# Layer 0's opening in a two-layer encoder trunk: squares and their sums placed behind the last input chunk, two weight units split into idle tiles, and another bank for the fourth projection block

## The chip, the cores and the metric

The kernel runs on one core of one Trainium2 chip. The metric is the device time of one execution in microseconds (us). The core has five engines: TensorE (PE; its weight loads are shown as PEld), VectorE (DVE), ScalarE (ACT), GpSimd (POOL) and SyncE (SP), which here only issues DMAs. Each engine works its own list of instructions in order and waits on semaphores for the others.

## The reference

Input x is 512 x 1024 (float32), the depth is 2. Cut to what matters here:

```python
for l in range(DEPTH):
    h = rmsnorm(x, attn_norm[l])                    # x * rsqrt(mean(x*x) + EPS) * g
    proj = jnp.einsum('bsd,de->bse', h, w_in[l])    # 1024 -> 6 x 512
    sb_q, sb_k, sb_v, df_q, df_k, df_v = jnp.split(proj, splits, axis=-1)
    sb_out = stick_breaking_attention(sb_q, sb_k, sb_v)          # 8 heads of 64
    dq, dk = rope(df_q, pos), rope(df_k, pos)
    df_out = rmsnorm(differential_attention(dq, dk, df_v, lam), subln_norm[l]) * (1.0 - lambda_init)
    x = x + jnp.einsum('bse,ed->bsd', concat([sb_out, df_out]), w_o[l])
    h = rmsnorm(x, mlp_norm[l])
    u = jnp.square(jax.nn.relu(jnp.einsum('bsd,df->bsf', h, w_ff1[l])))   # 1024 -> 4096
    x = x + jnp.einsum('bsf,fd->bsd', u, w_ff2[l])
return rmsnorm(x, final_norm)
```

## The kernel before, in words

**Layout.** x is held transposed: eight chunks of 128 features (partitions) by 512 tokens. The gain g is applied to x before the projections, and the factor rsqrt(mean) of each token is applied to the products when they are evicted from PSUM. So the projections need only x and g; the row `rbc` (the factors, on all partitions) is needed at the first eviction.

**Three products for one.** Each float32 operand is split into a high part (a rounded copy, type fp32r) and a low part (operand minus high part). `three` (L255 to L260) issues three matmuls for one: high by high (L258), and the two mixed ones (L259, L260). For x this split is `make_h` (L208 to L212): ScalarE writes h_hi (L209), VectorE h_lo (L210). For weights it is `split_part` (L110 to L119): ScalarE writes whi (L118), VectorE wlo (L119).

**Weights.** They come from HBM in units of 128 x 1024 in a fixed order: three raw buffers (pool wraw), and two pairs of split tiles (whi, wlo; pool wspl). A unit's DMA can be issued once the split that read its raw buffer is done, and a unit can be split once the matmuls that used its split tile are done. `W.next` splits two units ahead in program order. The first units of layer 0 are 0 and 1 (block d0, its q and k halves), 2 (w0v), 3 and 4 (d1q, d1k), 5 (w1v), 6 and 7 (d2), 8 (w2v).

**The opening of layer 0.** The DMAs of x's eight chunks and of quarters of units 0 and 1 are issued in turn. For each chunk ScalarE and VectorE make h and, for every second chunk, a quarter of both units. TensorE takes d0's two products together, chunk by chunk (48 matmuls into two banks), then block by block w0v, d1q, d1k, w1v and on (24 matmuls each). The sum of squares `ssq` is made beside it by `add_sq` (L214 to L223): ScalarE squares chunk 0 into ssq (L216) and each other chunk into a tile sq (L222), GpSimd adds sq to ssq (L223).

**The norm.** `rms_a` (L225 to L246) transposes ssq on TensorE (rs_a), reduces on VectorE (L230, L231), takes the power -0.5 on GpSimd (L236), splits the factors (chi, clo) and spreads them on diagonals (dgha, dgla: L241, L243). `rms_b` (L248 to L253) multiplies these with ones on TensorE (rb_a) and ScalarE copies the result to rbc. `RA` and `RB` count chunks of projections (a step is one `three`): in layer 0 rms_a is issued at step 21, rms_b at step 26. Until then finished blocks are held in their PSUM banks; after it cos_t and sin_t are multiplied by rbc, and the held blocks are evicted: `evict_d` (u, v, rotated on GpSimd L459 and L460, split, moved by DMAs on SP's queue L425 and copied by ScalarE L446 into the stacks st and kl) and `evict_v` (tv, transposed on TensorE as vT).

**Banks.** Three PSUM banks have the tag mm, two s, two t, one o. d0 and w0v take the three mm banks; the block that starts at step 24 (d1q) takes an s bank, and d1k waits for the bank of d0's q. The s banks later hold the attention scores.

**Attention** of layer 0 runs between the projections, shared out by cost. The scores S0d (L487, L488) use the s banks, which are free again when ScalarE has read them in the exponentials p0d (L540). md_hi and md_lo, four slices of 512 columns each, receive the differential heads after their norm.

**Order.** The order of instructions on each engine is made by a scheduler when the kernel is built, from the program order, its own costs and the dependencies.

Of the kernel before, what the change touches and what calls it, by code (L numbers as in the profile page):

```python
# [9 lines left out]
F32 = mybir.dt.float32  # L10
F32R = mybir.dt.float32r
BF16 = mybir.dt.bfloat16
AF = mybir.ActivationFunctionType
ALU = mybir.AluOpType
# [8 lines left out]
KC = D // P  # L23
# [8 lines left out]
LAG2, LAG3, KSB = 2, 3, 7  # L32
MTB = 1
FB = 6
SQP = False
RST = 2
WARM = 10
RA, RB, DLY_V = (21, 8), (26, 16), 3.5
MAN = ()
_CTX = {}  # L40
KC_GAP = 0.9
# [45 lines left out]
class _Weights:  # L87
    def __init__(self, nc, dram, rawp, splp):
        self.nc, self.dram, self.rawp, self.splp = nc, dram, rawp, splp
        self.loaded = self.split = self.used = 0  # L90
        self.raw, self.tiles = {}, {}
        self.depth = 3

    def parts(self, i):
# [14 lines left out]

    def split_part(self, i, a, b):  # L110
        nc = self.nc
        if i not in self.tiles:
            hi = self.splp.tile([P, 1024], F32R, tag="whi", name=f"whi{i}")
            lo = self.splp.tile([P, 1024], F32R, tag="wlo", name=f"wlo{i}")
            self.tiles[i] = (hi, lo)
        hi, lo = self.tiles[i]
        raw = self.raw[i]
        nc.scalar.activation(hi[:, a:b], raw[:, a:b], AF.Copy)  # L118
        nc.vector.tensor_tensor(out=lo[:, a:b], in0=raw[:, a:b], in1=hi[:, a:b].bitcast(F32), op=ALU.subtract)  # L119

    def do_split(self, n):
        while self.split < min(n, len(_UNITS)):
# [7 lines left out]
    def next(self, kind):  # L130
        i = self.used
        assert _UNITS[i][0] in kind
        self.used += 1
        if i > 0:
            self.do_split(i + 2)
        return self.tiles.pop(i)
# [3 lines left out]
def trunk(ctx, tc, xT, w, gains, lamv, cos, sin, out):  # L140
    nc = tc.nc
# [5 lines left out]
    def bank(tag, name, bufs=2):  # L147
        return ps.tile([P, 512], F32, tag=tag, name=name, bufs=bufs)
# [3 lines left out]
    W = _Weights(nc, w, wraw, wspl)  # L152
    cp.tile([P, 96], F32, tag="lead", name="lead")
    x = cp.tile([P, KC, S], F32, tag="x", name="x")
    h_hi = cp.tile([P, KC, S], F32R, tag="h_hi", name="h_hi")
    h_lo = cp.tile([P, KC, S], F32R, tag="h_lo", name="h_lo")
    ssq = cp.tile([P, S], F32, tag="ssq", name="ssq")
# [32 lines left out]
    def gcol(which, l, c):  # L190
        i = {"attn": l * 8, "mlp": 16 + l * 8, "final": 32, "sub": 40 + l}[which] + c
        return g_all[:, i : i + 1]
# [13 lines left out]
        nc.vector.tensor_tensor(out=lo, in0=src, in1=hi.bitcast(F32), op=ALU.subtract)  # L206

    def make_h(c, g):  # L208
        nc.scalar.activation(h_hi[:, c, :], x[:, c, :], AF.Copy, scale=g)  # L209
        nc.vector.scalar_tensor_tensor(  # L210
            out=h_lo[:, c, :], in0=x[:, c, :], scalar=g, in1=h_hi[:, c, :].bitcast(F32),
            op0=ALU.mult, op1=ALU.subtract)  # L212

    def add_sq(c, first, sqt, eng=nc.gpsimd, sqe=None):  # L214
        if first:
            nc.scalar.activation(ssq, x[:, c, :], AF.Square)  # L216
            return
        sq = sqt("sq")
        if sqe is not None:
            sqe.tensor_mul(sq, x[:, c, :], x[:, c, :])  # L220
        else:
            nc.scalar.activation(sq, x[:, c, :], AF.Square)  # L222
        eng.tensor_tensor(out=ssq, in0=ssq, in1=sq, op=ALU.add)  # L223

    def rms_a(src, inv_n, col, name, eng, dgt):  # L225
        pt = bank("t", "rs_" + name)
# [21 lines left out]
    def rms_b(bc, name, dg):  # L248
        dg_hi, dg_lo = dg
        pb = bank("t", "rb_" + name)  # L250
        nc.tensor.matmul(pb, ones_r.to_broadcast([P, P]), dg_hi, start=True, stop=False)
        nc.tensor.matmul(pb, ones_r.to_broadcast([P, P]), dg_lo, start=False, stop=True)
        nc.scalar.copy(bc, pb)  # L253

    def three(pt, a, b, first, last):  # L255
        ah, al = a
        bh, bl = b
        nc.tensor.matmul(pt, ah, bh, start=first, stop=False)  # L258
        nc.tensor.matmul(pt, ah, bl, start=False, stop=False)  # L259
        nc.tensor.matmul(pt, al, bh, start=False, stop=last)  # L260

    def hpair(c):
        return h_hi[:, c, :], h_lo[:, c, :]

    def wpair(u, c, n=P):
        return u[0][:, c * n : (c + 1) * n], u[1][:, c * n : (c + 1) * n]

    def block(name, tag="mm"):
        pt = bank(tag, name, 3 if tag == "mm" else 2)
        u = W.next("px" if name[0] == "p" else "1")  # L270
        for c in range(KC):
            three(pt, wpair(u, c), hpair(c), c == 0, c == KC - 1)
            yield pt if c == KC - 1 else None

    def constants(a2):
        nc.sync.dma_start(cos_t, cos)
        nc.sync.dma_start(sin_t, sin)
        lam_in = a2.tile([P, L * 4 * 64], F32, tag="t", name="lam_in", bufs=4)
        nc.sync.dma_start(lam_in, lamv.partition_broadcast(P))
        lam4 = lam_in.rearrange("p (l j d) -> p l j d", l=L, j=4)  # L280
        lam_pr = a2.tile([P, L, 2, 128], F32, tag="t", name="lam_pr", bufs=4)[:, :, :, 0:64]
        for l in range(L):
            for m in range(2):
                nc.vector.tensor_mul(lam_pr[:, l, m, :], lam4[:, l, 2 * m, :], lam4[:, l, 2 * m + 1, :])
                nc.vector.tensor_reduce(out=lam_sm[:, l, m : m + 1], in_=lam_pr[:, l, m, :], axis=AX.X, op=ALU.add)
        nc.scalar.activation(lam_ex.rearrange("p l m -> p (l m)"), lam_sm.rearrange("p l m -> p (l m)"), AF.Exp)
        for l in range(L):
            li = 0.8 - 0.6 * math.exp(-0.3 * l)
            nc.vector.tensor_sub(nlam[:, l : l + 1], lam_ex[:, l, 1:2], lam_ex[:, l, 0:1])
            nc.vector.tensor_scalar_add(nlam[:, l : l + 1], nlam[:, l : l + 1], -li)  # L290
            nc.vector.tensor_scalar_mul(gsub[:, l : l + 1], gcol("sub", l, 0), 1.0 - li)
# [57 lines left out]
    for l in range(L):  # L349
        with ExitStack() as actx:  # L350
# [3 lines left out]
            md_hi = ap_.tile([P, 4, S], F32R, tag="mdh", name=f"mdh{l}")  # L354
            md_lo = ap_.tile([P, 4, S], F32R, tag="mdl", name=f"mdl{l}")
# [19 lines left out]
            if l == 0:  # L375
                for c in range(KC):
                    if c % 2 == 0:
                        for i in range(2):
                            W.split_part(i, c * P, (c + 2) * P)
                    make_h(c, gcol("attn", 0, c))  # L380
                W.split = 2
                for c in range(KC):
                    add_sq(c, c == 0, tt, nc.gpsimd, nc.gpsimd if c % 2 and SQP else None)
                constants(a2)

            def evict_v(pt, kind, b, which):
# [306 lines left out]
            def dense():  # L693
                step, held = 0, []
                if l == 0:
                    b = int(ORDER[0][1])
                    us = [W.next("x"), W.next("x")]
                    pts = [bank("mm", f"p0{i}", 3) for i in range(2)]
                    for c, i in [(c, i) for c in range(5) for i in range(2)] + [(c, i) for i in range(2) for c in (5, 6, 7)]:
                        three(pts[i], wpair(us[i], c), hpair(c), c == 0, c == KC - 1)  # L700
                        step += 1
                        yield 3 * 0.216
                    held = [(pts[0], "d", b, "q"), (pts[1], "d", b, "k")]
                for item in ORDER[1 if l == 0 else 0 :]:
                    kind, b = item[0], int(item[1])
                    for which in ("qk" if kind in "ds" else "v"):
                        name = f"p{l}{kind}{b}{which}"
                        for pt in block(name, "s" if step == 24 else "mm"):
                            step += 1
                            if step == RA[l]:  # L710
                                dgs["a"] = rms_a(ssq, 1.0 / D, rcol, f"a{l}", nc.vector, tr)
                            if step == RB[l]:
                                rms_b(rbc, f"a{l}", dgs["a"])
                                nc.vector.tensor_mul(cos_t, cos_t, rbc)
                                nc.vector.tensor_mul(sin_t, sin_t, rbc)
                            yield 3 * 0.216
                        held.append((pt, kind, b, which))
                        if step >= RB[l]:
                            for args in held:
                                {"w": evict_v, "u": evict_v, "s": evict_s, "d": evict_d}[args[1]](*args)  # L720
                            held = []
                yield from wo(1)
# [4 lines left out]
            for cost in dense():  # L727
# [5 lines left out]
                while live and credit > 0:  # L733
                    c = next(at, None)
# [15 lines left out]
        with ExitStack() as fctx:  # L750
# [25 lines left out]
            for half in range(2):  # L776
                us = []
                for f in range(HC):
                    step = 0
# [6 lines left out]
                    if half == 0 and f == 0:  # L786
                        first = pt
# [5 lines left out]
                for db in range(KC):  # L793
                    pt = bank("mm", f"f2_{l}{half}{db}", 3)
                    for s in range(2):
                        u = W.next("2")
                        for f in range(n // 2):
                            g = s * (n // 2) + f
# [70 lines left out]
```

## Time and profile before

| | |
|---|---|
| time, median of 3 runs (lowest, highest) | 1233.09 us (1231.47, 1233.61) |
| time of the profiled execution | 1232.63 us |
| its span | 1230.8 us |
| granted TensorE clock, mean | 0.993 |
| busy: TensorE, VectorE, ScalarE, GpSimd | 1196.4, 683.6, 550.6, 210.9 us |
| GpSimd's additions L223 of the opening (7), busy | 10.1 us |
| the opening's h_lo L210 (8), busy | 9.5 us |
| d0's last matmul starts | 24.12 us |
| w0v's and d1q's last matmuls start | 31.13, 37.06 us |
| first exponential p0d | 59.05 us |

Busy time is the time in which an engine carries out instructions, and for TensorE it contains matmuls that run into each other. A row in order of time gives start, duration, engine, line, operation, what it writes and reads, and in brackets how long the engine was idle before it and who ended that wait. The waits are given as: who waited, for whom, total us, number, longest. The windows give the busy time of each engine between two times.

### The profile page before, as it was taken

The numbers are of one execution on the slowest core, as the hardware profiler recorded it, in microseconds if no ns is written. First come the engines' busy times: TensorE is split into PE (matmuls) and PEld (weight loads), VectorE is DVE, ScalarE is ACT, GpSimd is POOL, SyncE is SP. The second block draws the span as 40 slices with busy tenths as digits, with TensorE's granted clock in tenths as the row PEclk, the third lists the DMA queues.
The fourth block names the chain that finished last, engine by engine and source line by source line (L and its number), as shares of the span: only waits on it lengthen the run. The fifth ranks groups of instructions, "written<-read, shape, count | busy, mean of one in ns | idle before, by whom it ended". The sixth has DMA issues, their size and how long they took to land.

```text
span 1230.8 us, 15320 instructions
## 1 busy us (share of the span) xinstructions
PE 1196.4 (97%) x5658; PEld 989.4 (80%) x5658; DVE 683.6 (56%) x1009; ACT 550.6 (45%) x932; POOL 210.9 (17%) x267
## 2 busy tenths in 40 slices
PE   8999999999999999999998999999999999999996
PEld 4777888888888888888887788788888888888886
DVE  6687878765442244443367787887644323444325
ACT  5666566544332134333246765665443221433214
POOL 4223453230000000001123244432200000000002
PEclk9999999999999999999999999999999999999998
DMA  6444444123322323323324343432232233233221
GB/s 198 114 142 121 115 134 122 59 86 103 103 88 101 103 88 101 103 87 102 103 84 141 105 134 107 129 92 84 86 103 99 90 103 95 93 103 91 90 94 69
DMA packets 46890, 128.16 MB, mean 104 GB/s; under 512 B 7264, under 2 KB 10336, under 8 KB 46816
## 3 DMA queue, kind: packets, MB, share of 16 engines
q1 hardware_dynamic: 46672, 127.17, 33.8%
q8 instruction: 45, 0.74, 0.2%
q14 instruction: 29, 0.24, 0.1%
q10 hardware_dynamic: 144, 0.02, 0.0%
HBM read 104.09 MB, written 2.10 MB: 86 GB/s over the span
## 4 chain that ended last, share of the span: by engine, by line
PE 87%; DVE 4%; ACT 3%; POOL 2%; issue 1%; DMA 1%; SPq 0%; DVEq 0%; POOLq 0%; ACTq 0%
PE f L258 19%; PE f L259 19%; PE f L260 19%; PE wo L259 2%; PE wo L258 2%; PE wo L260 2%; DVE wlo L119 1%; PE T1s L568 1%; PE T0s L568 1%; ACT p0d L540 1%; PE O1s L597 0%; PE O0s L597 0%; PE O0s L596 0%; PE O1s L596 0%; PE S1d L487 0%
## 5 line engine op out<-in xcount | busy, mean ns | idle before, releaser
L118 ACT ACTIVATE whi<-raw 128x1024 fp32r<-128x1024 f32 (+2 forms) x200 | 205.1, 1027 | 493.3 <-PE f L259 427.6
L119 DVE TENSOR_TENSOR wlo<-raw,whi 128x1024 fp32r<-128x1024 f32 (+2 forms) x200 | 247.7, 1239 | 151.6 <-ACT whi L118 150.5
L258 PE MATMUL f<-h_hi,whi 128*128 128x512 f32 x512 | 199.4, 389 | 0.0
L260 PE MATMUL f<-h_hi,wlo 128*128 128x512 f32 x512 | 199.2, 389 | 0.0
L259 PE MATMUL f<-h_lo,whi 128*128 128x512 f32 x512 | 199.2, 389 | 0.0
L258 PE MATMUL f<-uh,whi 128*128 128x512 f32 x496 | 192.9, 389 | 0.0
L259 PE MATMUL f<-ul,whi 128*128 128x512 f32 x496 | 192.9, 389 | 0.0
L260 PE MATMUL f<-uh,wlo 128*128 128x512 f32 x496 | 192.9, 389 | 0.0
L771 DVE SCALAR_TENSOR_TENSOR ft<-f,rbc 128x512 f32<-128x512 f32 x64 | 44.3, 692 | 163.9 <-PE f L260 163.0
L258 PEld LDWEIGHTS f<-h_hi,whi 128*128 128x128 f32 x512 | 96.1, 188 | 20.0
L260 PEld LDWEIGHTS f<-h_hi,wlo 128*128 128x128 f32 x512 | 96.1, 188 | 20.0
L259 PEld LDWEIGHTS f<-h_lo,whi 128*128 128x128 f32 x512 | 96.1, 188 | 19.8
L223 POOL TENSOR_TENSOR ssq<-ssq,sq 128x512 f32<-128x512 f32 x28 | 44.5, 1591 | 382.1 <-ACT sq L222 372.7
L260 PEld LDWEIGHTS f<-uh,wlo 128*128 128x128 f32 x496 | 93.1, 188 | 19.5
L258 PEld LDWEIGHTS f<-uh,whi 128*128 128x128 f32 x496 | 93.1, 188 | 19.3
L259 PEld LDWEIGHTS f<-ul,whi 128*128 128x128 f32 x496 | 93.1, 188 | 19.2
L800 DVE TENSOR_TENSOR x<-x,f 128x512 f32<-128x512 f32 x32 | 22.0, 688 | 103.0 <-PE f L260 103.0
L340 POOL TENSOR_TENSOR ssq<-ssq,sqf 128x256 f32<-128x256 f32 x6 | 4.4, 738 | 338.4 <-ACT sqf L338 335.0
L206 DVE TENSOR_TENSOR ul<-fu,uh 128x512 fp32r<-128x512 f32 x64 | 44.1, 692 | 0.4 <-ACT uh L205 0.4
L205 ACT ACTIVATE uh<-fu 128x512 fp32r<-128x512 f32 x64 | 40.6, 634 | 2.0
L772 ACT ACTIVATE fu<-ft 128x512 f32<-128x512 f32 x64 | 39.6, 618 | 1.6 <-DVE ft L771 1.6
L508 POOL TENSOR_TENSOR sig0s<-sig0s,C0s 128x128 f32<-128x128 f32 (+3 forms) x32 | 30.1, 939 | 55.0 <-DVE C0s L505 39.0
(722 smaller groups left out, 2164.9 us busy)
## 6 DMA issues: line engine op xcount, KB each, us to landing
raw<-in_w SPq DMA_DIRECT2D x176, 512.0 KB, 3.4
raw<-in_w SPq DMA_DIRECT2D x16, 448.0 KB, 3.2
x<-in_xT SPq DMA_DIRECT2D x8, 256.0 KB, 4.5
out_xT<-y SPq DMA_DIRECT2D x8, 256.0 KB, 2.4
raw<-in_w SPq DMA_DIRECT2D x8, 128.0 KB, 4.5
cos_t<-in_cos SPq DMA_DIRECT2D x2, 256.0 KB, 4.2
sin_t<-in_sin SPq DMA_DIRECT2D x2, 256.0 KB, 4.3
kl0d0k<-l0d0k SPq DMA_DIRECT2D x8, 64.0 KB, 2.2
```

What stands on the lines that cost most here:

```text
L118: nc.scalar.activation(hi[:, a:b], raw[:, a:b], AF.Copy)
L119: nc.vector.tensor_tensor(out=lo[:, a:b], in0=raw[:, a:b], in1=hi[:, a:b].bitcast(F32), op=ALU.subtract)
L205: nc.scalar.activation(hi, src, AF.Copy)
L206: nc.vector.tensor_tensor(out=lo, in0=src, in1=hi.bitcast(F32), op=ALU.subtract)
L223: eng.tensor_tensor(out=ssq, in0=ssq, in1=sq, op=ALU.add)
L258: nc.tensor.matmul(pt, ah, bh, start=first, stop=False)
L259: nc.tensor.matmul(pt, ah, bl, start=False, stop=False)
L260: nc.tensor.matmul(pt, al, bh, start=False, stop=last)
L508: nc.gpsimd.tensor_mul(sig[:, 0:wd], sig[:, 0:wd], C[:, 1 : wd + 1])
L568: nc.tensor.transpose(pt[:, off : off + P], u["w"][qi][:, kb * P : (kb + 1) * P], ident)
L771: nc.vector.scalar_tensor_tensor(out=t, in0=pt, scalar=0.0, in1=rbc, op0=ALU.max, op1=ALU.mult)
L772: nc.scalar.activation(uu, t, AF.Square)
```

## The change

The seven additions of squares in layer 0's opening go from GpSimd to VectorE. `behind` writes order dependencies without a semaphore: the first square stands behind the last h_hi on ScalarE, the first addition behind the last h_lo on VectorE, the squares are kept in their order, and the third square and second addition stand behind the split of unit 2. Units 2 and 3 are split within the opening, and their split tiles are the two halves of md_hi and md_lo of layer 0 (`home`) instead of whi and wlo. rms_b of layer 0 is issued at step 30 instead of 26. The block that starts at step 32 (d1k) takes an s bank too. The switch SQP, which was off, is removed. Layer 1 and the other uses of `add_sq` keep GpSimd.

```diff
-SQP = False
-RA, RB, DLY_V = (21, 8), (26, 16), 3.5
+RA, RB, DLY_V = (21, 8), (30, 16), 3.5
...
-        self.raw, self.tiles = {}, {}
+        self.raw, self.tiles, self.home = {}, {}, {}
...
     def split_part(self, i, a, b):
         nc = self.nc
+        if i not in self.tiles and i in self.home:
+            self.tiles[i] = self.home[i]
         if i not in self.tiles:
...
-        nc.scalar.activation(hi[:, a:b], raw[:, a:b], AF.Copy)
-        nc.vector.tensor_tensor(out=lo[:, a:b], in0=raw[:, a:b], in1=hi[:, a:b].bitcast(F32), op=ALU.subtract)
+        h = nc.scalar.activation(hi[:, a:b], raw[:, a:b], AF.Copy)
+        self.last = h, nc.vector.tensor_tensor(
+            out=lo[:, a:b], in0=raw[:, a:b], in1=hi[:, a:b].bitcast(F32), op=ALU.subtract)
...
+    def behind(a, b):
+        tc.add_manual_dep(a.ins, b.ins.name, mybir.DependencyInfo(
+            mybir.DependencyClass.NoSync, mybir.DependencyReason.DATA), reason="order")
...
-                    make_h(c, gcol("attn", 0, c))
+                    ends = make_h(c, gcol("attn", 0, c))
                 W.split = 2
-                for c in range(KC):
-                    add_sq(c, c == 0, tt, nc.gpsimd, nc.gpsimd if c % 2 and SQP else None)
+                for i in range(2):
+                    W.home[2 + i] = tuple(
+                        m[:, 2 * i : 2 * i + 2, :].rearrange("p e t -> p (e t)") for m in (md_hi, md_lo))
+                squares = [add_sq(c, c == 0, tt, nc.vector) for c in range(KC)]
+                behind(squares[0][0], ends[0])
+                behind(squares[1][1], ends[1])
+                for a, b in zip(squares[1:], squares):
+                    behind(a[0], b[0])
+                W.do_split(3)
+                behind(squares[2][0], W.last[0])
+                behind(squares[2][1], W.last[1])
+                W.do_split(4)
                 constants(a2)
...
-                        for pt in block(name, "s" if step == 24 else "mm"):
+                        for pt in block(name, "s" if step in (24, 32) else "mm"):
```

`add_sq` and `make_h` now return their two instructions, so that `behind` can name them.

More of the change, by code (lines that the diff above doesn't have):

```diff
@@ L208, in make_h, with add_sq @@
     def make_h(c, g):
-        nc.scalar.activation(h_hi[:, c, :], x[:, c, :], AF.Copy, scale=g)
-        nc.vector.scalar_tensor_tensor(
+        a = nc.scalar.activation(h_hi[:, c, :], x[:, c, :], AF.Copy, scale=g)
+        return a, nc.vector.scalar_tensor_tensor(
             out=h_lo[:, c, :], in0=x[:, c, :], scalar=g, in1=h_hi[:, c, :].bitcast(F32),
             op0=ALU.mult, op1=ALU.subtract)
-    def add_sq(c, first, sqt, eng=nc.gpsimd, sqe=None):
+    def add_sq(c, first, sqt, eng=nc.gpsimd):
         if first:
-            nc.scalar.activation(ssq, x[:, c, :], AF.Square)
-            return
+            return nc.scalar.activation(ssq, x[:, c, :], AF.Square), None
         sq = sqt("sq")
[L219 to L223, printed above, removed]
+        s = nc.scalar.activation(sq, x[:, c, :], AF.Square)
+        return s, eng.tensor_tensor(out=ssq, in0=ssq, in1=sq, op=ALU.add)
+    def behind(a, b):
+        tc.add_manual_dep(a.ins, b.ins.name, mybir.DependencyInfo(
+            mybir.DependencyClass.NoSync, mybir.DependencyReason.DATA), reason="order")
     def rms_a(src, inv_n, col, name, eng, dgt):
```

## The prediction

> **What bounds the kernel now.** I read the page first: TensorE is busy for 97% of the span, so an edit pays only where TensorE stands still or runs on late operands. The windows by stage come next, then the order in time of each engine from 0 to 65 us.
>
> ```profile
> PE 1196.4 (97%) x5658; PEld 989.4 (80%) x5658; DVE 683.6 (56%) x1009; ACT 550.6 (45%) x932; POOL 210.9 (17%) x267
> ```
> Windows of the opening (busy us of PE, PEld, DVE, ACT, POOL; granted clock; DMA share; GB/s):
> ```profile
> 5.00:10.00 5.00, 4.13 (x15) 2.21 (x13) 3.09 (x5) 3.86 (x9) 1.40 (x3) 1.00 1.01 356
> 10.00:15.00 5.00, 3.81 (x13) 2.24 (x13) 5.00 (x6) 5.00 (x11) 4.07 (x3) 1.00 1.00 349
> 15.00:20.00 5.00, 2.85 (x8) 1.75 (x9) 5.00 (x4) 1.80 (x4) 4.69 (x4) 0.87 0.04 16
> 20.00:25.00 5.00, 4.97 (x21) 3.78 (x19) 1.84 (x5) 1.13 (x2) 0.00 (x0) 0.79 0.47 159
> ```
> VectorE is full from 10 to 20 us, and input transfers are over at 15 us (the DMA share falls to 0.04): the second half of the opening waits for VectorE, not for data. VectorE and GpSimd in time:
> ```profile
> 7.67 0.75 DVE L210 SCALAR_TENSOR_TENSOR h_lo<-x,g_all,h_hi 128x512 fp32r<-128x512 f32 x1 [1.43 <-ACT h_hi L209]
> 14.18 2.92 DVE L119 TENSOR_TENSOR wlo<-raw,whi 128x256 fp32r<-128x256 f32 x2
> 17.02 3.45 DVE L210 SCALAR_TENSOR_TENSOR h_lo<-x,g_all,h_hi 128x512 fp32r<-128x512 f32 x2
> 21.07 0.74 DVE L210 SCALAR_TENSOR_TENSOR h_lo<-x,g_all,h_hi 128x512 fp32r<-128x512 f32 x1
> 12.41 7.52 POOL L223 TENSOR_TENSOR ssq<-ssq,sq 128x512 f32<-128x512 f32 x5 [0.80 <-ACT sq L222]
> ```
> The same h_lo takes 0.74 us alone and 1.7 us while GpSimd adds squares; the two wlo take 2.92 us together there and 0.75 at 20.39, after GpSimd stopped. So the additions stretch VectorE. Then the chain and the waits:
> ```profile
> 18.84 0.79 PE p L259
> 23.87 1.07 ACT whi L118
> 24.96 1.24 DVE wlo L119
> 26.24 0.50 PE p0w0v L260
> ```
> ```profile
> PE S0d L487 <- ACT p0d L540: 6.7, 5, 2.2
> PE p L260 <- DVE wlo L119: 1.9, 3, 0.9
> PE p L259 <- DVE h_lo L210: 1.5, 3, 1.0
> ```
> The last h_lo lets TensorE go on at 18.84 and 21.8; d0's 48 matmuls end at 24.1. Only then is unit 2 split (its tiles are those of unit 0), and w0v's third matmul waits until 26.24. Later waits are for softmax (S0d), in layer 0's attention.
>
> **The sum, step by step.** Pitches from back-to-back rows: matmul 0.2275, h_hi 0.61, square 0.52, whi of 1024 0.96 (1.06 long), wlo of 1024 1.13 (1.22 long), h_lo and 512-wide VectorE operations 0.60 (0.69 long; 0.72 where one addition must wait for the one before).
>
> *Removed:* seven GpSimd additions (10.1 us busy) and seven squares between ScalarE's h_hi. The eight h_lo fall from 9.5 us to about 6 (8 x 0.74), the eight 256-wide wlo from 6.4 to about 3. Both engines then follow the transfers. x chunk 7 is issued at 8.88; x took 2.9 to 5.0 us to land, median 4.5: 13.4 (bounds 11.8 and 13.9). Its h_hi lasts to 14.1, h_lo to 14.85; six matmuls stand behind that in the built order, so d0 ends near 16.2 (24.1 before). If the DMA order moves, up to 0.5 us either way.
>
> *Added behind the last chunk:* ScalarE does squares 0 and 1 (2 x 0.52), then unit 2's high half at 15.05 to 16.1 (its transfer, issued at 9.48, is inside the DMA stretch that ends near 15). VectorE's low half follows to 17.36; the first sum ends at 15.7 in front of it and costs nothing. The tiles are md_hi and md_lo, first written in before by a head's norm at 118.19 (mdh), so there is no wait for a tile; in wspl's two buffers unit 2 waits for d0's end (7.1 us of idle ScalarE at 23.87). w0v's third matmul goes at 17.4, 0.6 us after TensorE reaches it; 22 matmuls end w0v at 22.4, against 31.36. **Lead 8.9 us.**
>
> Unit 3's high half stands behind five squares: 16.0 + 5 x 0.52 = 18.6, to 19.7. Its transfer is issued when raw0 is split (about 13.5, with 3.5 to landing). VectorE: sums 2 to 5 from 17.3 to 20.1, unit 3's low half to 21.3, sum 6 to 21.9, unit 4's low half to 23.0, sum 7 to 23.65. The rs_a transposes now stand after two chunks of d1q: 22.4 + 6 x 0.2275 = 23.8. They just fit; each us later on VectorE costs a us here. On SP's queue, sin and the lambda vectors now stand behind weight loads. The lambda transfer waits for sum 4 (19.4) and took 4.5: 23.95. Its eight small VectorE operations (1.1 us) stand in front of L230: 25.05. L230 and L231 take to 25.95, GpSimd's power 1.08, during which unit 5's low half runs to 27.2; chi, clo and dgha end at 28.2. TensorE is at rb_a at 24.15 + 15 x 0.2275 = 27.55 and waits 0.7. d1q ends at 29.5 (37.28 before): **lead 7.8**. RB = 30 moves rb_a behind seven of d1q's eight chunks; at 26 it would stand next to rs_a and wait some 4 us. Dropping SQP, which was off, costs nothing.
>
> *Evictions:* rbc starts at 29.5 against 33.38, a lead of only 3.9, and so for what hangs on it. d1k takes the second "s" bank and doesn't wait for d0q's bank. The v transposes need tv0w (39.25 - 3.9 = 35.35); TensorE is there after 23 matmuls at 34.7 and waits 0.7. d1k ends at 36.1, **lead 7.1**; w1v ends at 41.55, d2q's S0d comes near 46.2. The d0 stack moves: first issue 40.48 - 3.9 = 36.6, sixteen at some 0.63, landing 2.2: 48.3 at the latest, for the last S0d half near 49. Fits; the first score's bank, from d1k, is free at 40.6.
>
> *ScalarE then:* 36.0 + two h0d0k 1.26, two whi 1.96, two vdh 1.2, sixteen copies at 0.64 = 10.2, two h0d1k 1.26, whi 0.96 = 52.9 to the first exp, if it never waits (before: 59.05, with a 2.0 us wait for GpSimd's u0d1q at 50.02; my order puts that at 41.8, ahead of need). The S0d that waited until 59.89 goes at 52.9 + 0.84 = 53.75: **lead 6.1**. Behind that the built order differs up to about 127 us, with no operation more or less, then it is the same, with TensorE full, so the lead stays. What the reordering does to the 4 us of idle TensorE between 60 and 130 I bound at 1.5 each way and take as nothing.
>
> The clock: between 19 and 22 us the granted clock was 0.50 (part of the 0.87 and 0.79 above), after a stretch of 3.4 us with five matmuls in it; matmuls came at 0.43. My opening has no such sparse stretch after 7.5 us, so I charge none. One would cost up to half of 3.4 = 1.7 us. [...]
>
> The profiled execution took 1232.63 (span 1230.8); its span less 6.1 is 1224.7, its time 1226.5. The median of the three runs is 0.46 higher, so I give 1227.0.
>
> **Rivals.** (a) *The lead of the evictions decides.* ScalarE waits for GpSimd's u0d1q again, as at 50.02, and everything follows rbc: gain 3.9, 1229.2; with a cold clock stretch 1.7 less than 6.1, 4.4: 1228.7. For: that wait was on the chain. Against: d1k's products now stand earlier in VectorE's order. Chance 0.17. (b) *The whole lead lives:* the lambdas land early, the 0.7 us waits at rb_a and tv0w go, ScalarE has slack: 8.9, 1224.2. Against: three waits of mine lie within a us. Chance 0.14. (c) *No change:* the S0d waits take it all back, 1233. These waits have their cause in ScalarE, whose work is not less; but it starts 3.9 us earlier at least. 0.06. (d) *Slower:* the new order of layer 0's attention lengthens each softmax wait. In it two whi splits stand together in front of an exp (2 x 0.96). If each of the five S0d waits grew by 1.9, that is 9.5 us, 3.4 more than the lead: 1236.5. It decides from 1.2 us on each. Against: only one such pair is seen. 0.05. That the change doesn't do what it says is ruled out by the built order: no addition is left on GpSimd in the opening. Forecast (gain 4.5 to 8): 0.58.
>
> **The numbers.** 0.2% (2.5 us) is about what a measurement of this kernel tells from none. Forecast, (a) and (b) are faster by more: 0.58 + 0.17 + 0.14 = 0.89; within 0.2%, (c): 0.06; slower, (d): 0.05. The range runs from (b) with the early landing of chunk 7, 1223.5, to a gain of 2.6, 1230.5; outside lie (c), (d) and some edges, about 0.15.
>
> **What would show it.** Right: h_lo at 0.74 throughout; d0's last matmul near 16, w0v's near 22.4; rs_a about 24; rbc near 29.5; first p0d exp near 53; granted clock 1.00 to 30 us; MLP stages unchanged in length. Wrong: TensorE waiting over a us at rs_a or rb_a, a clock of 0.50 in the opening, or S0d waits over 8 us in all in the first 130 us.

## The result, and the profile after

The changed kernel takes 1227.99 us (median; 1226.19 to 1228.74), the kernel before 1233.42 on the same chip: ratio 0.995, 95% interval 0.9939 to 0.996, which is a gain of 4.9 to 7.5 us. The forecast was 1227.0 (1223.5 to 1230.5), faster. The profiled execution takes 1228.06 us with a span of 1226.3, 4.6 us less than the 1232.63 before, at the same mean clock of 0.993.

Line numbers are two higher after the edits in the opening and twelve higher in the attention. First the page, then the windows of the opening (busy us of PE, PEld, DVE, ACT, POOL; granted clock; DMA share; GB/s):

```profile
PE 1194.8 (97%) x5658; PEld 991.6 (81%) x5658; DVE 680.1 (55%) x1016; ACT 551.6 (45%) x932; POOL 202.3 (16%) x260
```
```profile
5.00:10.00 5.00, 4.95 (x17) 3.31 (x16) 3.54 (x8) 3.50 (x7) 0.00 (x0) 1.00 1.01 367
10.00:15.00 5.00, 5.00 (x24) 4.12 (x23) 4.71 (x10) 4.85 (x11) 0.00 (x0) 1.00 0.89 313
15.00:20.00 5.00, 5.00 (x24) 4.14 (x23) 4.43 (x7) 5.00 (x9) 0.00 (x0) 1.00 0.94 349
20.00:25.00 5.00, 5.00 (x26) 4.17 (x25) 4.44 (x12) 1.97 (x3) 0.00 (x0) 1.00 0.65 199
```

TensorE is full from 10 us on, at clock 1.00; before it had 3.81 and 2.85 busy us in the second and third row. The transfers run on to 25 us, because units 2 and 3 are split early and their raw buffers are loaded again. In order of time:

```profile
11.64 1.42 DVE L212 SCALAR_TENSOR_TENSOR h_lo<-x,g_all,h_hi 128x512 fp32r<-128x512 f32 x2
13.71 0.75 DVE L212 SCALAR_TENSOR_TENSOR h_lo<-x,g_all,h_hi 128x512 fp32r<-128x512 f32 x1
16.84 3.08 DVE L221 TENSOR_TENSOR ssq<-ssq,sq 128x512 f32<-128x512 f32 x4
...
17.35 0.39 PE L262 MATMUL p<-h_hi,wlo 128*128 128x512 f32 x1
17.58 0.39 PE L260 MATMUL p0w0v<-h_hi,mdh 128*128 128x512 f32 x1
```

Each h_lo takes 0.7 us, as alone; the last is done at 14.5. d0's last matmul still starts only at 17.35, and w0v follows at the next pitch, without a wait. The norm then, engine by engine, and TensorE's waits up to 130 us:

```profile
26.01 2.05 POOL L238 TENSOR_TENSOR rcol<-ms,mhalf 128x4 f32<-128x4 f32 x1 [23.72 <-DVE nlam L292]
25.96 1.22 DVE L120 TENSOR_TENSOR wlo<-raw,whi 128x1024 fp32r<-128x1024 f32 x1
28.09 0.17 DVE L239 CAST chi<-rcol 128x4 fp32r<-128x4 f32 x1 [0.92 <-POOL rcol L238]
29.21 0.47 PE L253 MATMUL rb_a<-dgha,ones_r 128*128 128x512 f32 x1 [0.78 <-DVE dgha L243]
30.42 0.59 ACT L255 COPY rbc<-rb_a 128x512 f32<-128x512 f32 x1 [5.73 <-PE rb_a L254]
```
```profile
PE S0d L499 <- ACT p0d L552: 6.3, 5, 2.2
...
PE rb_a L253 <- DVE dgha L243: 0.8, 1, 0.8
PE vT0w L405 <- DVE tv0w L400: 0.6, 1, 0.6
```

The waits of d0's products for h_lo and wlo are gone. The power takes 2.05 us beside the low half of unit 5, twice its time before (1.08). The waits for softmax are about as long as before (6.3 against 6.7), but something new stands behind two of them. Windows of the attention and of the same place in layer 1, and the two rows of TensorE that end the two waits:

```profile
60.00:70.00 10.00, 6.78 (x38) 5.07 (x36) 7.49 (x16) 7.88 (x15) 2.72 (x3) 1.00 0.66 217
70.00:80.00 10.00, 9.02 (x41) 8.03 (x42) 7.63 (x21) 7.46 (x20) 1.92 (x3) 0.83 0.51 148
90.00:100.00 10.00, 7.67 (x36) 5.78 (x35) 8.29 (x21) 6.90 (x17) 5.39 (x5) 0.94 0.38 112
100.00:110.00 10.00, 10.00 (x48) 8.45 (x47) 9.46 (x16) 7.16 (x12) 4.51 (x4) 0.89 0.48 130
650.00:660.00 10.00, 8.21 (x32) 6.98 (x33) 6.37 (x20) 8.55 (x21) 1.84 (x3) 0.83 0.53 154
```
```profile
70.98 0.44 PE L499 MATMUL S0d<-st0d1k,st0d1q 128*128 128x384 f32 x1 [2.01 <-ACT p0d L552]
98.61 0.70 PE L499 MATMUL S0d<-st0d2k,st0d2q 128*128 128x512 f32 x1 [2.16 <-ACT p0d L552]
```

After the waits of 2.01 and 2.16 us the granted clock is halved for 3.4 us each (0.17 of one window of 10 us; 0.06 and 0.11 of two). Before, all windows from 60 to 130 us stood at 1.00, for example:

```profile
70.00:80.00 10.00, 9.53 (x49) 7.51 (x50) 8.46 (x23) 9.85 (x23) 2.04 (x3) 1.00 0.37 92
100.00:110.00 10.00, 7.90 (x41) 6.62 (x42) 7.83 (x18) 9.53 (x19) 4.90 (x5) 1.00 0.52 145
```

The stretch in layer 1, behind a softmax wait of 2.99 us, is not new: the kernel before has it from 657.0 us on.

Matmul start times give the lead of after over before, stage by stage:

| start of | before | after | lead | forecast |
|---|---|---|---|---|
| w0v's last matmul | 31.13 | 22.79 | 8.3 | 8.9 |
| d1k's first | 37.28 | 30.44 | 6.8 | 7.8 |
| rbc (ScalarE) | 33.38 | 30.42 | 3.0 | 3.9 |
| w1v's first | 43.20 | 37.14 | 6.1 | 7.1 |
| first exponential | 59.05 | 53.80 | 5.3 | 6.1 |
| w2v's first | 64.02 | 56.41 | 7.6 | |
| s1q's first | 128.89 | 124.54 | 4.4 | 6.1 |

From s1q on it stays: the end is 4.6 us earlier.

### The profile page after: what moved, and what is told of

Read it like the earlier page. It is cut to its first block, busy times and chain, and to the rows that moved or that the text cites. A ratio compares the mean times of both kernels' runs of the same rounds, so it can differ in the third digit from the quotient of the medians.

```text
span 1226.3 us, 15312 instructions
## 1 busy us (share of the span) xinstructions
PE 1194.8 (97%) x5658; PEld 991.6 (81%) x5658; DVE 680.1 (55%) x1016; ACT 551.6 (45%) x932; POOL 202.3 (16%) x260
## 4 chain that ended last, share of the span: by engine, by line
PE 85%; DVE 4%; ACT 3%; POOL 2%; issue 1%; SPq 1%; DMA 0%; DVEq 0%; POOLq 0%; ACTq 0%
PE f L260 19%; PE f L262 19%; PE f L261 19%; PE wo L261 2%; PE wo L260 2%; PE wo L262 2%; DVE wlo L120 1%; SPq L437 1%; PE T1s L580 1%; PE T0s L580 1%; PE O1s L609 0%; PE O0s L609 0%; PE O1s L608 0%; PE O0s L608 0%; PE S1d L499 0%
## 5 line engine op out<-in xcount | busy, mean ns | idle before, releaser
L120 DVE TENSOR_TENSOR wlo<-raw,whi 128x1024 fp32r<-128x1024 f32 (+2 forms) x198 | 242.0, 1224 | 147.1 <-ACT whi L119 146.2
L221 POOL TENSOR_TENSOR ssq<-ssq,sq 128x512 f32<-128x512 f32 x21 | 34.8, 1656 | 374.3 <-ACT sq L220 365.2
L520 POOL TENSOR_TENSOR sig1s<-sig1s,C1s 128x128 f32<-128x128 f32 (+3 forms) x32 | 30.0, 939 | 55.3 <-DVE C1s L517 40.9
```

Source lines behind the costliest of these rows:

```text
L120: self.last = h, nc.vector.tensor_tensor(out=lo[:, a:b], in0=raw[:, a:b], in1=hi[:, a:b].bitcast(F32), op=ALU.subtract)
L221: return s, eng.tensor_tensor(out=ssq, in0=ssq, in1=sq, op=ALU.add)
L520: nc.gpsimd.tensor_mul(sig[:, 0:wd], sig[:, 0:wd], C[:, 1 : wd + 1])
```

## Experiments, first part: which part of the change carries the gain

These four ran on one chip beside the kernel before at 1234.07 us. Theory: the additions slowed h_lo, and the early splits let TensorE go on at once; both are needed. Rivals: the additions alone, or the tiles alone.

**Sums only.** No early splits, RB 26, one bank less:

```diff
-RA, RB, DLY_V = (21, 8), (30, 16), 3.5
+RA, RB, DLY_V = (21, 8), (26, 16), 3.5
...
-                for i in range(2):
-                    W.home[2 + i] = ...
...
-                W.do_split(3)
-                behind(squares[2][0], W.last[0])
-                behind(squares[2][1], W.last[1])
-                W.do_split(4)
...
-                        for pt in block(name, "s" if step in (24, 32) else "mm"):
+                        for pt in block(name, "s" if step == 24 else "mm"):
```

> Of the change, only the squares and sums behind the last chunk with the sums on VectorE; no tiles for units 2 and 3, RB 26, d1k in an mm bank. Theory P (GpSimd's additions stretch VectorE, and that is most of the gain): the eight h_lo take 0.74 us each, d0's last matmul starts near 17.4 as in the changed kernel; unit 2's low half stands behind six sums, so w0v's third matmul comes near 20.4 and w0v ends near 25.4; rb_a stands earlier and rbc starts near 28.1. Gain 4 to 5.5 us against before (1228 to 1229.5). Rival T (most of the gain is that w0v no longer waits for d0's tiles): gain under 2.5, above 1231.

Measured: 1231.85 us, ratio 0.9982 (0.9972 to 0.9993), 2.2 less than before. TensorE's waits:

```profile
PE vT0w L398 <- DVE tv0w L393: 1.7, 1, 1.7
PE p0w0v L260 <- ACT whi L119: 1.5, 1, 1.5
```

d0 ends as in the changed kernel (its last matmul starts at 17.03), but unit 2 has to wait for d0's tiles, and its low half stands on VectorE behind six sums. w0v's third matmul starts at 20.66, near the 20.4 forecast, but behind these waits the granted clock is 0.50 from 20.5 to 23.9 us, and the four transposes rs_a stand inside w0v: its last matmul starts at 27.54, not near 25.4 (22.79 in the changed kernel). Most of the opening's lead is lost right there. The forecast of 4 to 5.5 us was missed. The time lies in the range of rival T, but the next run speaks against T's cause.

**Tiles only.** The additions stay on GpSimd as before; units 2 and 3 get the idle tiles; RB 26, one bank less:

```diff
-                squares = [add_sq(c, c == 0, tt, nc.vector) for c in range(KC)]
-                behind(squares[0][0], ends[0])
...
+                for c in range(KC):
+                    add_sq(c, c == 0, tt, nc.gpsimd)
                 W.do_split(4)
```

> Of the change, only the split of units 2 and 3 into md_hi and md_lo; squares and sums between the chunks with the sums on GpSimd as before, RB 26, d1k in an mm bank. Theory P: d0's last matmul stays near 24.1; only w0v's waits at 24.98 and 26.24 go, 1.3 to 1.8 us: 1231.6 to 1232.1. Rival T: gain over 3 us, below 1230.4.

Measured: 1235.51 us, 1.0013 (1.0005 to 1.0022): slightly slower.

```profile
PE S0d L493 <- ACT p0d L546: 8.9, 6, 3.1
PE p L262 <- DVE wlo L120: 1.9, 3, 0.9
PE p L261 <- DVE h_lo L212: 1.7, 4, 0.9
```

Both ranges were missed. The waits for h_lo and wlo are those of before. d0's last matmul starts at 23.15 and not at 24.12; in this opening the clock stays at 1.00. The lead of 2.1 us at w0v's end is more than taken in the attention: the waits for softmax are 2.2 us longer than before, and the clock is 0.50 from 60.1 to 63.5 us.

**The sums behind the last chunk, but on GpSimd** (all else as in the change):

```diff
-                squares = [add_sq(c, c == 0, tt, nc.vector) for c in range(KC)]
+                squares = [add_sq(c, c == 0, tt, nc.gpsimd) for c in range(KC)]
```

> The changed kernel with the seven sums given back to GpSimd, still behind the last chunk. Theory P (place): the opening is as in the changed kernel (d0's last matmul near 17.4), but seven additions at 1.33 to 1.5 us end near 25, the transposes rs_a stand inside w0v and TensorE waits 3 to 4 us there, and the splits of units 2 to 4 on VectorE are stretched; gain 1 to 3 us, 1230.4 to 1232.4. Rival V (placing them behind the chunk is all, the engine doesn't matter): as the changed kernel within 1 us, 1227 to 1229.

Measured: 1232.89 us, 0.9994 (0.9984 to 1.0004): no difference that can be told.

```profile
PE rs_a L231 <- POOL ssq L221: 5.5, 1, 5.5
```

So moving the additions out of h_lo's way is enough for d0 (its last matmul starts at 17.43). But on GpSimd they last until 27.1, and TensorE stands 5.5 us at rs_a, after 15 of w0v's 24 matmuls, and then runs at clock 0.50 from 25.6 to 32.4 us. The wait was forecast as 3 to 4 us, the halved clock not at all, and the time is 0.5 us above the range. VectorE's 0.7 us for each addition is what closes the norm in time.

**Without the bank for d1k:**

```diff
-                        for pt in block(name, "s" if step in (24, 32) else "mm"):
+                        for pt in block(name, "s" if step == 24 else "mm"):
```

> The changed kernel with d1k in an mm bank again. Theory B: d1k must wait until d0's q has been read (VectorE's v0d0q, 33.5) although TensorE is there at 30.4: 3.1 us of wait, of which the 0.6 us at the v transposes is given back: 2 to 3 us slower than the changed kernel, 1230 to 1231. Rival E (what hangs on rbc decides anyway): less than 1 us slower, 1228 to 1229.

Measured: 1229.27 us, 0.9971 (0.996 to 0.9983).

```profile
PE p0d1k L260 <- DVE v0d0q L464: 3.1, 1, 3.1
```

The bank saves a wait of 3.1 us and a stretch at clock 0.50 behind it (33.1 to 36.5 us), yet the changed kernel is only some 1.3 faster by its median, between the two forecasts. d1k starts 3.2 us later here, the first exponential 1.6, s1q 1.3; in the attention this kernel has one halved stretch (67.3 us) where the changed one has two.

Sums alone give 2.2 us, tiles alone minus 1.4; both together, without the bank, 4.8. The sum of the parts would be 0.8: the two need each other. These are totals: each of these kernels got its own built order in the attention, so they are not prices of the opening alone.

## Experiments, second part: RB, the power, and the halved clock

In these kernels but the first, the built order of the changed kernel is written into the kernel as order dependencies for all engines, so that an edit moves nothing else (no run holds the order fixed without an edit; that this alone costs nothing is assumed). Their line numbers are about 190 higher. The kernel before stood at 1232.57, 1232.94 and 1233.03 us beside them.

**RB at 26 again.**

```diff
-RA, RB, DLY_V = (21, 8), (30, 16), 3.5
+RA, RB, DLY_V = (21, 8), (26, 16), 3.5
```

> The changed kernel with RB at 26 again. The prediction said that rb_a would then stand next to rs_a and TensorE would wait some 4 us (time 1231 to 1232). Rival: the number does nothing. In the built order of the two kernels every instruction of every engine stands at the same place, because the scheduler puts rb_a where its operand is due and not where the count says. Then the rb_a wait is 0.8 us and the time that of the changed kernel, 1228 within 0.5.

Measured: 1227.81 us, 0.996 (0.9948 to 0.9971); rb_a waits 0.8 us, as in the changed kernel. The number does nothing here, and the 4 us of my prediction for it were wrong: the scheduler decides where rb_a stands.

**Unit 5's low half behind the diagonal products.** VectorE's order:

```diff
-wlo (unit 5)
 chi
 clo
 dgha
 dgla
+wlo (unit 5)
```

> The changed kernel with its whole order held fixed and one instruction moved: the low half of unit 5 stands behind the two diagonal products (dgha, dgla) on VectorE and no longer beside GpSimd's power. Theory (the power took 2.05 us because a two-input VectorE operation ran beside it): the power takes 1.0 to 1.2 us, chi starts near 27.1, the 0.8 us wait at rb_a goes, rbc starts near 29.6 instead of 30.42. If that lead lives to the end the time is 1227.2, 0.8 less than the changed kernel; if the evictions or softmax take it back, it is the same within 0.3. Rival (the power itself takes 2 us when it starts later, or the clock of GpSimd differs from execution to execution): the power stays at 2 us, chi at 28.1, no change.

Measured: 1225.52 us, 0.9943 (0.9931 to 0.9955). In order of time:

```profile
25.78 1.03 POOL L428 TENSOR_TENSOR rcol<-ms,mhalf 128x4 f32<-128x4 f32 x1 [23.48 <-DVE nlam L482]
26.84 0.17 DVE L429 CAST chi<-rcol 128x4 fp32r<-128x4 f32 x1 [1.03 <-POOL rcol L428]
28.04 0.39 PE L443 MATMUL rb_a<-dgha,ones_r 128*128 128x512 f32 x1
28.33 1.22 DVE L294 TENSOR_TENSOR wlo<-raw,whi 128x1024 fp32r<-128x1024 f32 x1
```

The power takes 1.03 us, the wait at rb_a is gone, rbc starts at 29.15 instead of 30.42. The gain is larger than this 1.3 us: at s1q's first matmul it is 2.6, because w2v to s1q takes 66.8 us instead of 68.1. That rest is the clock:

```profile
70.00:80.00 10.00, 10.00 (x53) 8.45 (x53) 9.26 (x23) 7.59 (x18) 2.24 (x4) 1.00 0.46 138
90.00:100.00 10.00, 7.72 (x34) 6.22 (x35) 8.40 (x18) 6.85 (x15) 4.27 (x4) 0.83 0.46 131
```
```profile
69.73 0.44 PE L689 MATMUL S0d<-st0d1k,st0d1q 128*128 128x384 f32 x1 [2.01 <-ACT p0d L742]
```

The same wait of 2.01 us, with the same instructions before and behind it but 1.25 us earlier, is not followed by a halved clock. The wait of 2.16 us still is.

**Three waits filled** with matmuls whose weights are zero, added to sums that are open anyway:

```diff
+    def fill(pt, n, width):
+        last = None
+        for _ in range(n):
+            z = nc.tensor.matmul(pt, zeros[:, 0:128], zeros[:, 128 : 128 + width], start=False, stop=False)
...
+            if last is not None:
+                behind(z, last)
+            last = z
```

> The changed kernel with its whole order held fixed, and matmuls with zero weights put into three waits for softmax in the attention: 16 of 256 columns before the first scores of d1's third row block (a wait of 2.0 us), 8 of 512 columns before those of d2's last block (2.2 us), 12 of 512 columns before those of layer 1's d0 third block (3.0 us). They add zeros to sums that are open anyway. Theory (what was given back in the attention is the halved clock of 3.4 us behind each of those waits, 1.7 us each): clock 1.00 from 60 to 130 us and from 640 to 680, the lead of 7.6 us at w2v's first matmul falls by less than 1 us until s1q's, and the time is 1228.0 - 3 x 1.7 = 1223 (1222.5 to 1225), with less spread from execution to execution. Rival (ScalarE's exponentials set the pace there, so faster matmuls only wait longer for the next one): clock 1.00 but S0d waits longer by as much, time 1227.5 to 1228.5. Second rival (the filling matmuls run past the waits and delay the scores): up to 1 us slower.

Measured: 1229.69 us, 0.9971 (0.9961 to 0.9982): 1.7 to 1.9 slower than the changed kernel.

```profile
70.00:80.00 10.00, 9.53 (x52) 8.16 (x52) 8.99 (x22) 7.36 (x20) 1.92 (x3) 1.00 0.47 145
90.00:100.00 10.00, 9.34 (x48) 6.59 (x48) 8.70 (x19) 7.06 (x15) 3.78 (x4) 1.00 0.49 138
650.00:660.00 10.00, 9.47 (x33) 5.74 (x35) 4.75 (x15) 5.21 (x14) 1.77 (x3) 0.69 0.40 111
```
```profile
650.29 0.69 PE L705 MATMUL S1d<-st1d0k,st1d0q 128*128 128x384 f32 x1 [3.00 <-ACT p1d L758]
...
651.54 4.81 PE L469 MATMUL p1d2q<-edge 128*128 128x512 bf16 x11 [0.24 <-issue]
```

In layer 0 the halved clock is gone, and w2v to s1q takes 1.1 us less than in the changed kernel; for the first wait that need not be the filling, since the kernel with unit 5 moved lost its halved stretch there without any. In layer 1 my edit went wrong: the filling stood behind the scores, not in front, so the wait of 3.00 us stayed and the filling ran behind it, mostly at the halved clock, for 4.8 us. The filling before d2's last block also held up w3v's end and so a later transpose (waits at vT0w 2.4 us instead of 0.6).

**Both edits together.**

> The two edits together: unit 5's low half behind the diagonal products, and the three waits filled. If both theories hold and the gains add, 1222.2; if the 0.8 us of the power is taken back in the attention, 1223; if neither holds, 1228.

Measured: 1229.3 us, 0.9974 (0.9964 to 0.9983). It carries the same misplaced filling, so it says nothing of the sum of the two gains.

**The filling in place:** only in the first of the two waits of layer 0 and in layer 1's. In the list that fixes TensorE's order each filling now follows the matmul that stands ahead of the waiting scores.

```diff
         row = [every[e][k] for a, n in runs for k in range(a, a + n)]
+        row = [j for i in row for j in [i] + AFTER.get(i.name, [])]
```

> The changed kernel, its order held fixed, with matmuls with zero weights only in the two waits where the filled kernel tells nothing yet or told it plainly: 16 of 256 columns before the first scores of d1's third row block, and 12 of 512 columns before the scores of layer 1's d0 third block, this time held in front of those scores (in the filled kernel they stood behind them and ran at half clock, 4.8 us). Nothing is put before d2's last block, where the filling held up w3v's eviction. Theory (each wait of 2 to 3 us costs a further 1.7 us by the 3.4 us of halved clock behind it): clock 1.00 in 70 to 80 us and in 650 to 660, lead up by some 1.4 us behind the first (as in the filled kernel) and by 1.7 behind the second, time 1228.0 - 3.1 = 1225 (1224 to 1226.5). Rival (the exponentials set the pace; the clock is no matter): 1227.5 to 1228.5.

Measured: 1225.5 us, 0.9941 (0.9928 to 0.9953), as forecast; five runs lie between 1224.97 and 1226.23.

```profile
70.00:80.00 10.00, 9.76 (x52) 8.12 (x51) 8.98 (x22) 7.35 (x19) 1.92 (x3) 1.00 0.49 144
650.00:660.00 10.00, 9.92 (x47) 8.01 (x48) 9.49 (x24) 7.22 (x17) 2.88 (x4) 1.00 0.52 158
```

w2v to s1q is 1.4 us shorter than in the changed kernel, but it was as short without filling when unit 5 was moved, so this trace doesn't show that the first filling did it. By the medians, 2.5 us, some 1.4 are left beside layer 1's share. Layer 1 gives 1.1 more (d1k's first matmul there is 1.95 earlier, the end 3.1), and here the cause is clear: every kernel whose wait of 3.0 us there was left open shows the halved clock behind it. In the 10 us from 650 us on the granted clock was 0.83 in the changed kernel, with RB at 26 and with both edits together, 0.88 with unit 5 moved and 0.69 with the filling behind the scores; in the kernel before it was 0.50 from 657.0 to 660.4 us; in the four kernels of the first part it was 0.99 on the mean from 620 to 850 us, as in the changed kernel. The rival that only the exponentials set the pace falls there.

**Real matmuls in the waits** instead of zeros: nine of s0q's in front of d2's last scores, twelve of d2q's in front of layer 1's; unit 5 later and zeros in the first wait.

> What the other runs point to: the kernel with unit 5's low half behind the diagonal products, the zero matmuls in the first wait, and real matmuls in the two others: nine of s0q's are moved in front of the last scores of d2, twelve of d2q's in front of layer 1's scores of d0's third block. Theory: the moved matmuls take up to 2.0 and 2.7 us of the waits and the halved clock behind each goes (1.7 us each), less what later scores wait instead. If nothing is given back 1225.5 - 8 = 1217.5; if later scores wait for the same exponentials and only the clock is won, 1225.5 - 3.4 = 1222. I take 1221 (1218 to 1224). Rival (the softmax sets the pace, clock or not): 1225 to 1226.

Measured: 1226.83 us, 0.995 (0.9937 to 0.9964): slower than unit 5 alone and outside the forecast.

```profile
PE vT0w L605 <- DVE tv0w L600: 4.2, 2, 3.6
PE S0d L699 <- ACT p0d L752: 2.3, 4, 1.7
```
```profile
102.56 0.68 DVE L600 TENSOR_TENSOR tv0w<-p0w3v,rbc 128x512 f32<-128x512 f32 x1
```

The waits for scores shrink from 6.3 to 2.3 us, but TensorE now comes early to the transposes of w3v, and their operand stands on VectorE behind the softmax operations of the same scores. It waits 3.6 us there, with the clock halved behind it (0.83 from 100 to 110 us). In layer 1 three shorter waits, the longest 1.0 us, are left, and a halved stretch still follows at 654.2. The wait was moved, not removed.

**What held, together:** unit 5 later, zeros in the first wait and in layer 1's.

> The two edits that held, together: unit 5's low half behind the diagonal products, and zero matmuls in the first wait of layer 0 and in layer 1's, held in front of the scores. If the gains add (0.8 to 1.3 us from the power, 1.35 from the first wait, 1.7 from layer 1's), 1228.0 - 4.1 = 1224 or a little less. If the clock behind the first wait was the same gain that the kernel with unit 5 moved already had by chance (it showed no halved clock there), only layer 1's 1.7 comes on top of its 1225.5: 1223.8. The two agree within 0.3; what tells them apart from a rival is that nothing is added: 1225.5.

Measured: 1224.49 us, 0.9932 (0.9918 to 0.9946), the fastest kernel here. Over the kernel with unit 5 moved it wins 1.0, over the changed kernel about 3.5. The clock was at 1.00 from 70 to 80 us in the kernel with unit 5 moved, too, so only layer 1's filling adds, and the zeros in layer 0 add nothing that can be seen: 632.07 against 631.84 at d1k's first matmul there, 1222.8 against 1223.7 at the end.

## Why the prediction was right, and where its sizes were off

**Right:** h_lo at 0.7 throughout, no clock of 0.50 in the opening, w0v's end (23.0, a pitch behind its last start at 22.79, for 22.4), rs_a without a wait (24.38 for 23.8), the waits at rb_a (0.78 for 0.7) and at tv0w (0.62 for 0.7), softmax waits under 8 us. By the medians the gain is 5.4, inside the 4.5 to 8 given to the forecast. The rival that all of the 8.9 lives fell at rbc. Rival (a), the evictions' lead alone, was a gain of 3.9, or 4.4 with a cold clock: the profiles' 4.6 lies next to the second number, but not by its mechanism, since u0d1q ended no wait and the halved clock came elsewhere.

ScalarE's sum held best: from the first h0d0k to the first exponential 16.9 us were forecast and 17.0 measured (36.83 to 53.80), with no wait over 0.2. So the 0.9 us that are missing at the first exponential are those that were missing at rbc, and when unit 5 was moved the 1.27 us won at rbc came through as 1.26 at the first exponential.

**d0's end: 17.6, not 16.2.** The step counted six matmuls behind the last h_lo. That was done at 14.5, even earlier than forecast, but thirteen were still to start: TensorE was behind. It began at 5.24, and its first fifteen matmuls took 4.8 us, where the pitch of 0.2275 would give 3.4; the 33 others followed at that pitch from 10.08. So the wait of 0.6 us that I put at w0v's third matmul did not come, and of the 1.4 us 0.6 were left at w0v's end.

**The power: 2.05, not 1.08.** That row was taken from a place where no large VectorE operation with two inputs ran beside it but in its last 0.2 us, and the same sentence put one there (unit 5's low half). This costs 0.97 us at chi. TensorE came to rb_a at 28.4 instead of 27.55, so the wait there came out right by chance, both sides being 0.9 later. Moving that one operation showed it: 1.03 us, rbc 1.27 us earlier. The prediction had told of h_lo stretched by GpSimd (from 0.74 to 1.7 us), but did not turn it round.

**RB.** The statement on 26 was about a place in the program, not in the built order; the run shows no difference.

**The attention: taken as nothing, plus or minus 1.5.** Between the first exponential and s1q 0.9 us of the lead were lost. The waits for softmax stayed about the same in length, but behind two of them the clock was halved for 3.4 us. The price was in the text, up to 1.7 us each, yet considered for the opening alone, where it did not occur. One such stretch fewer between w2v and s1q went with 1.35 us (unit 5 moved); filling layer 1's wait gained 1.1. Idle TensorE between 60 and 130 us was 5.4 us in the windows before, not 4.

**The bank** was counted as a wait avoided, rightly, but the 3.1 us are worth 1.3. rbc starts at the same time with and without it (30.42, 30.40), and without it of the 3.2 us at d1k's start 1.6 are left at the first exponential and 1.3 at s1q.

The median of the gain (5.4) is larger than that of the profiled pair (4.6) because the profiled execution of the kernel before (1232.63) was 0.8 faster than the median of its runs beside the changed kernel (1233.42). What stays open is why executions of one kernel differ. Halved stretches that fall or do not fall on a wait may be a part of it, but the mean clocks do not show it: the changed kernel's fastest execution, 1226.19, had 0.997 and others near 1228 had 0.993, yet 1226.58 had 0.994, and in the kernel with the filling in place the slowest of five, 1226.23, had 0.997.

## What to carry to other kernels

A stall that several engines share goes only when each is served: here the sums without the tiles gave 2.2 us, the tiles without the sums minus 1.4, both 4.8. When a step is moved, look at what runs beside it in its new place, on both engines, and take its duration from a row with such a neighbour (the power took 1.08 us without and 2.05 with one). Count the backlog of the engine that is to be fed, not only the arrival of its last operand, and price a wait with the slower clock that may stand behind it (here 3.4 us at 0.50 behind waits of 2.01 to 2.99 us).

## What the runs showed of the hardware

**GpSimd's power took longer beside VectorE, too.** The power on 128x4 took 1.08 us in the kernel before and 1.03 when unit 5 was moved, and 2.05 beside a two-input VectorE operation of 1.22 us that had begun 0.05 us earlier; it ended 0.9 us after it, which is nearly its own time. In the kernel before, two smaller operations ran beside it:

```profile
27.07 1.08 POOL L236 TENSOR_TENSOR rcol<-ms,mhalf 128x4 f32<-128x4 f32 x1 [7.15 <-DVE ms L231]
27.43 0.35 DVE L284 TENSOR_TENSOR lam_pr<-lam_in 128x64 f32<-128x64 f32 x2
```

These two small two-input operations of VectorE ran in the middle of the power's 1.08 us and took 0.35 us together, as at 23.84 us in the changed kernel, where no power ran. So this power did not lengthen them, as far as the profile's rough times for GpSimd tell.

**Behind waits of 2 to 3 us the granted clock was halved, but not behind each.** In the changed kernel waits of 2.01, 2.16 and 2.99 us were followed by 3.4 us at 0.50, from 71.4, 98.7 and 651.7 us on (the waits end at 71.0, 98.6 and 651.8). The same 2.01 us, 1.25 us earlier with unit 5 moved, was not: the clock was 1.00 in each us from 66 to 73. Nor was a wait of 2.23 us that ends at 102.1 us in the kernel before, with 1.00 from 100 to 110 us. What decides is not shown by any run here. Since the halved stretch was missing with unit 5 moved without any filling, the first filling's own gain can't be told from the shift of the program in time.

Twelve matmuls with zero weights, held in front of the waiting scores in layer 1's wait of 3.0 us, went with a clock of 1.00 from 650 to 660 us; standing behind the scores they ran for 4.8 us, mostly at half clock (0.69 in those 10 us).
